# Splitting 80 weight pieces instead of 64 during the attention, in place and in four tiles

## The chip, the cores and the metric

The kernel runs on one core of a Trainium2 chip. The metric is the device time of one execution in microseconds (us), as the median of several runs. Engines are named TensorE (PE in the rows), VectorE (DVE), ScalarE (ACT), GpSimd (POOL) and SyncE (SP, which only issues DMAs); PEld is TensorE's weight load.

## The reference

One layer of a hybrid encoder is applied to a prompt of 1024 tokens and to a sample of 256, each behind 16 learned tokens. The core of it:

```
p = rms_norm(h) @ w_in
c_q, c_kv, k_rope, u = split(p)
o_attn = mla(c_q, c_kv, k_rope, ...)      # 4 heads, softmax over all keys
o_hy   = hyena(u, conv_w, filters, bias)  # order 2: z = x_n * (conv(z, f_n) + bias_n * z)
mix = concat(rms_norm(o_attn), rms_norm(o_hy)) @ w_o
h = h + rms_norm(mix)
m = square(relu(rms_norm(h) @ w_ff1)) @ w_ff2
h = h + rms_norm(m)
```

The widths are 1024 for the model and 4096 for the MLP. All is float32, so `w_o`, `w_ff1` and `w_ff2` are the large weights.

## The kernel before

A float32 product is made as three TensorE products of rounded numbers (`mm3`, L257 to L261): high by high, high by low, low by high. For a weight piece of 128x512 numbers (256 KB) ScalarE casts the high part (`hi`, L267), and GpSimd or VectorE subtracts it from the piece for the low part (`lo`, L270). L273 and L276 are the helpers for other elementwise work of VectorE and GpSimd.

Three stages follow one another. The first makes the projections and the filters (until about 395 us). The second is the attention (to about 612 us), with the sample's convolution in its last units and behind it (to about 690 us). The third is the prompt's hyena convolution, into which the sample's output projection and MLP are woven, and then the prompt's own output projection and MLP.

The attention runs in units, one for 128 queries of one head: 4 heads by 10 query tiles, 8 of the prompt and 2 of the sample. A unit i issues the scores of its tile on TensorE, the row maximum `nmx` on VectorE (L994) and the exponential `prob` on ScalarE (L999). Between these stand the transposes of unit i - 1's probabilities, whose high part `pth` is cast by ScalarE and whose low part `ptl` is subtracted by VectorE, in two groups of 128x512 and a third of 128x128. Two tiles of queries make a pair; their weighted sum `po` is made in parts in the following units, and its result `ot` is stored (`oa`). Steps of the next head's projections (`kh`, `pv`) fill the rest.

Beside it, `presplit` (L361 to L389) makes low parts of weight pieces that the sample path will use later: 16 of `w_o`, then of `w_ff1` and `w_ff2` in the order of their use. SP loads a piece (`pre_raw`, L370), ScalarE casts the high part, GpSimd subtracts the low part, and SP stores the low part to DRAM (`lo_...`, L375). High and low part share a tile, `pre_lo`, of which there are two, so a cast waits until the store of the piece two before has landed. Each unit from the first to the 32nd takes two steps, so 64 pieces are done after 32 units. Later, `ring` (L391) brings each weight piece of the sample path: for a piece with a stored low part it loads the piece and the low part (`w_lo` from DRAM) and casts the high part; for any other it loads the piece and lets GpSimd subtract (`w_lo<-w_raw,w_hi`).

On TensorE, ScalarE and VectorE the attention's instructions keep the order in which the code writes them (`pin`, L1161), except for the sample's convolution (`loose`, L1150). GpSimd's and SP's instructions are placed by a scheduler.

Of the kernel before, what the change touches and what calls it, by code (L numbers as in the profile page):

```python
# [13 lines left out]
F32 = mybir.dt.float32  # L14
F32R = mybir.dt.float32r
# [6 lines left out]
P = 128  # L22
# [154 lines left out]
def mk(ap, dims):  # L177
    return bass.AP(tensor=ap.tensor, offset=ap.offset, ap=[ap.ap[0]] + [list(d) for d in dims])


def f(ap):
    return ap.bitcast(F32)
# [15 lines left out]
def run(gen):  # L198
    for _ in gen:
        pass  # L200
# [32 lines left out]
class Builder:  # L233
# [127 lines left out]
    def presplit(self, pool, n):  # L361
        nc = self.nc
        keys = list(self.sample_pieces())[:n]
        raws, last = {}, None

        def load(k):
            if k < n:
                raw = raws[k] = pool.tile([P, 512], F32, name="pre_raw", bufs=2)
                src = self.piece(*keys[k])
                nc.sync.dma_start(raw.rearrange("p (a b) -> p a b", a=4) if len(src.shape) == 3 else raw, src)  # L370

        def store():
            if last is not None:
                d = self.d_lo[last[0]] = self.dr.tile([P, 512], F32, name="lo_" + "_".join(map(str, last[0])))
                nc.sync.dma_start(d, f(last[1]))  # L375

        load(0)
        load(1)
        yield
        for k in range(n):  # L380
            raw = raws.pop(k)
            t = pool.tile([P, 512], F32R, name="pre_lo", bufs=2)
            self.hi(t, raw)
            self.lo(t, raw, t, nc.gpsimd)
            store()
            last = keys[k], t
            load(k + 2)
            yield
        store()  # L389

    def ring(self, pool, src, bufs, rp=None, every=0, key=None):  # L391
        nc = self.nc
# [503 lines left out]
    def phase_b(self):  # L896
        tc, nc, a = self.tc, self.nc, self.a
# [3 lines left out]
        with ExitStack() as st:  # L901
# [5 lines left out]
            wk = self.pool(st, "b_work", 2)  # L907
# [122 lines left out]
            def weigh(h, t, qp, pth, ptl, rcs):  # L1030
                vh, vl = t[4:]
                nb, b0 = (8, 0) if qp < 4 else (2, 8)
                po = pv.tile([P, 512], F32, name="po", bufs=1)
                o = po[:, :256]
                for b in range(nb):
                    if b == nb // 2:
                        yield
                    self.mm3(o, vh[:, b0 + b], vl[:, b0 + b], pth[:, b], ptl[:, b], b == 0, False)
                b = 8 if qp < 4 else 10
                self.mm3(o, vh[:, b], vl[:, b], pth[:, 8], ptl[:, 8], False, True)  # L1040
                for i in range(2):
                    nc.tensor.transpose(po[:, 256 + i * 128:384 + i * 128], mk(rcs[i], [[0, 128]]), self.ident)
                yield
                rb = wk.tile([P, 256], F32, name="rb")
                nc.scalar.copy(rb, po[:, 256:])
                ot = wk.tile([P, 256], F32, name="ot")
                self.tt(ot, o, rb, ALU.mult)
                (nc.gpsimd if h >= self.dbg.get("oq", 4) else nc.sync).dma_start(self.d_oa[h][:, qp * 256:qp * 256 + 256], ot)
                yield
# [4 lines left out]
            with self.hp(4):  # L1054
                self.hi(krh[0:64], self.ka[0:64])
                self.lo(krl[0:64], self.ka[0:64], krh[0:64])
                raw, rk = stage(TM), stage(T)
                nc.sync.dma_start(rk[64:128], self.ka[0:64])
                nc.sync.dma_start(raw[64:128], self.qr[0:64])
                self.hi(krh[64:128], rk[64:128])  # L1060
                self.lo(krl[64:128], rk[64:128], krh[64:128])
                self.hi(qst[0][0:64], self.qr[0:64])
                self.hi(qst[0][64:128], raw[64:128])
                self.lo(qst[0][64:128], raw[64:128], qst[0][64:128])
                self.ropes.close()
                hps.append(self.pool(st, "b_head1"))
                pre_st = st.enter_context(ExitStack())
                pre = self.presplit(self.pool(pre_st, "b_pre"), 64)
                next(pre)
                for _ in range(self.dbg.get("n6", 6)):  # L1070
                    next(prep, None)
# [15 lines left out]
            n = len(units)  # L1087
# [4 lines left out]
            for i in range(n + 3):  # L1092
                start = len(nc.cur_bb.bb.instructions)
                sm = tn = nothing
                if i < n:
                    h, qt = units[i]
                    if i % 10 == 2 and h + 1 < NH:
                        for _ in prep:
                            pass
                        prep = head_prep(h + 1, heads[h + 1]) if h else early  # L1100
                    prob[i] = []
                    sm = softmax(heads[h], h, qt * 128, qt < 8, sets[qt % 2], reads[qt % 2], prob[i])
                if i == 33:

                    run(pre)
                    pre_st.close()
                    self.low.close()
                    self.wr = self.pool(self.rest, "f_w", 4, side="right")
                    sz = self.pool(self.sz_stack, "sz", 1, side="right")
                    self.conv_constants()  # L1110
                    conv = self.hyena_sample(cp, sz, lambda: pv.tile([P, 512], F32, name="pv"))
                next(sm, None)
                self.loose(conv)
                if 0 < i <= n:
                    h, qt = units[i - 1]
                    pair = (i - 1) // 2
                    if qt % 2 == 0:
                        pts[pair] = (wk.tile([P, 9, 256], F32R, name="pth"), wk.tile([P, 9, 256], F32R, name="ptl"), [])
                    p, rc = prob.pop(i - 1)
                    pts[pair][2].append(rc)  # L1120
                    tn = turn(p, sets[qt % 2], reads[qt % 2], qt < 8, *pts[pair][:2], qt % 2)
                next(tn, None)
                self.loose(conv)
                next(sm, None)
                if i >= 3 and i % 2 == 1:
                    h, qt = units[i - 3]
                    weighing = weigh(h, heads[h], qt // 2, *pts.pop((i - 3) // 2))
                next(weighing, None)
                if i > 0:
                    next(pre, None)  # L1130
                next(tn, None)
                self.loose(conv)
                if i % 2 == 0:
                    next(weighing, None)
                next(prep, None)
                if i > 0:
                    next(pre, None)
                if i == 0:
                    next(prep, None)
                if self.dbg.get("c4", 0):  # L1140
                    self.loose(conv)
                if i == n + 2:
                    a0 = len(nc.cur_bb.bb.instructions)
                    run(conv)
                    if self.dbg.get("lo", 1):
                        self.free.update(x.name for x in nc.cur_bb.bb.instructions[a0:])
                if self.dbg.get("pin", 1):
                    self.pin(start)
# [760 lines left out]
```

## Time and profile before

| | |
|---|---|
| median of 3 runs | 1961.19 us (1959.61 to 1962.14) |
| profiled execution | 1959.85 us, its span 1958.1 us |
| TensorE busy | 1787.0 us, 91% |
| VectorE busy | 1189.3 us, 61% |
| ScalarE busy | 773.8 us, 40% |
| GpSimd busy | 648.1 us, 33% |
| `w_lo` subtractions on GpSimd | 292, 414.8 us |
| `pre_lo` subtractions on GpSimd | 64, 81.9 us |

Busy times are sums over the whole span. They say which engine is nearest to its bound on average; which one sets the end in a stage is read from that stage's waits. An instruction's bracket tells how long its engine sat idle before it, and what ended that.

### The profile page before, as it was taken

Reading aid. Unit: us, or ns where it says so; the run is one execution under the profiler, and the core shown is the slowest. Engines: PE = TensorE matmul, PEld = TensorE weight load, DVE = VectorE, ACT = ScalarE, POOL = GpSimd, SP = SyncE. Lnnn points to the kernel's source line nnn. Section 1 sums busy time; section 2 is a strip of 40 time slices with the busy share of each in tenths; the row PEclk is TensorE's granted clock in tenths of the full one; section 3 lists DMA queues with packets and bytes.
Section 4 is the critical chain, followed back from the end, with each engine's and each line's share of the span. In section 5 each row is a group of like instructions: output and inputs, shape, how many; then the busy total and the mean of one; then the engine's idle time right before and its main releaser. Section 6 shows DMA issues by size and latency. Waiting matters only on the chain. (4 is left out here: it accounts for less than half of the span.)

```text
span 1958.1 us, 26574 instructions
## 1 busy us (share of the span) xinstructions
PE 1787.0 (91%) x9806; PEld 1566.5 (80%) x9806; DVE 1189.3 (61%) x1958; ACT 773.8 (40%) x1378; POOL 648.1 (33%) x556
## 2 busy tenths in 40 slices
PE   7999999889887987998889899899999999999996
PEld 6898999778776776887769778677888888888885
DVE  6589885755455858999752865764343333333346
ACT  6444343365554444332254565554322222222232
POOL 3221212344452210124466762234422222222234
PEclk9999998999999989999989989899999999999998
DMA  4454535356566266764443564335211111111104
GB/s 164 149 178 151 178 111 177 95 170 192 176 202 218 78 235 208 258 218 142 154 147 121 178 225 147 120 112 192 96 50 44 44 43 44 50 52 55 59 1 140
DMA packets 173669, 263.10 MB, mean 134 GB/s; under 512 B 14491, under 2 KB 85089, under 8 KB 173411
## 3 DMA queue, kind: packets, MB, share of 16 engines
q1 hardware_dynamic: 164952, 242.38, 38.4%
q0 software_dynamic: 5872, 17.06, 2.9%
q10 hardware_dynamic: 2714, 1.96, 0.3%
q8 instruction: 77, 1.26, 0.3%
q14 instruction: 54, 0.43, 0.1%
HBM read 202.51 MB, written 56.18 MB: 132 GB/s over the span
## 5 line engine op out<-in xcount | busy, mean ns | idle before, releaser
L270 POOL TENSOR_TENSOR w_lo<-w_raw,w_hi 128x512 fp32r<-128x512 f32 x292 | 414.8, 1433 | 705.3 <-ACT w_hi L267 638.7
L267 ACT CAST w_hi<-w_raw 128x512 fp32r<-128x512 f32 x388 | 237.8, 619 | 444.2 <-PE p L260 289.8
L259 PE MATMUL p<-a2h,w_hi 128*128 128x512 f32 (+1 forms) x784 | 283.8, 362 | 15.1 <-ACT w_hi L267 7.8
L259 PE MATMUL p<-sh,w_hi 128*128 128x512 f32 (+1 forms) x800 | 285.6, 361 | 11.0 <-DVE acc L273 6.0
L260 PE MATMUL p<-sl,w_hi 128*128 128x512 f32 (+1 forms) x800 | 283.4, 354 | 8.4 <-DVE sl L270 8.4
L261 PE MATMUL p<-a2h,w_lo 128*128 128x512 f32 (+1 forms) x784 | 281.6, 359 | 7.6 <-POOL w_lo L270 7.6
L261 PE MATMUL p<-sh,w_lo 128*128 128x512 f32 (+1 forms) x800 | 283.6, 355 | 0.0
L260 PE MATMUL p<-a2l,w_hi 128*128 128x512 f32 (+1 forms) x784 | 279.9, 357 | 0.3
L273 DVE TENSOR_TENSOR acc<-acc,p 128x512 f32<-128x512 f32 (+1 forms) x284 | 184.8, 656 | 147.4 <-PE p L261 147.0
L259 PEld LDWEIGHTS p<-sh,w_hi 128*128 128x128 f32 x800 | 154.5, 194 | 35.6 <-ACT sh L267 6.1
L259 PEld LDWEIGHTS p<-a2h,w_hi 128*128 128x128 f32 x784 | 151.8, 194 | 38.1 <-ACT w_hi L267 10.7
L260 PEld LDWEIGHTS p<-sl,w_hi 128*128 128x128 f32 x800 | 155.5, 194 | 31.7 <-DVE sl L270 11.0
L261 PEld LDWEIGHTS p<-a2h,w_lo 128*128 128x128 f32 x784 | 152.1, 194 | 31.5 <-POOL w_lo L270 9.8
L261 PEld LDWEIGHTS p<-sh,w_lo 128*128 128x128 f32 x800 | 155.3, 194 | 21.0
L260 PEld LDWEIGHTS p<-a2l,w_hi 128*128 128x128 f32 x784 | 151.9, 194 | 22.5 <-DVE a2l L276 0.7
L276 DVE SCALAR_TENSOR_TENSOR rl<-p,rs 128x512 f32<-128x512 f32 (+1 forms) x66 | 44.5, 674 | 199.7 <-PE p L261 199.6
L1769 ACT ACTIVATE rl<-rl 128x512 f32<-128x512 f32 (+1 forms) x66 | 40.8, 619 | 236.4 <-DVE rl L276 236.4
L259 PE MATMUL pp<-ah,w_hi 128*128 128x432 f32 x336 | 123.6, 368 | 0.0
L261 PE MATMUL pp<-ah,w_lo 128*128 128x432 f32 x336 | 122.0, 363 | 0.0
L260 PE MATMUL pp<-al,w_hi 128*128 128x432 f32 x336 | 121.9, 363 | 0.0
L270 POOL TENSOR_TENSOR pre_lo<-pre_raw,pre_lo 128x512 fp32r<-128x512 f32 x64 | 81.9, 1282 | 102.7 <-ACT pre_lo L267 102.3
L270 DVE TENSOR_TENSOR ptl<-sset,pth 128x512 fp32r<-128x512 f32 (+2 forms) x112 | 59.0, 527 | 84.0 <-ACT pth L267 83.8
(383 smaller groups left out, 3793.8 us busy)
## 6 DMA issues: line engine op xcount, KB each, us to landing
w_raw<-in_w_ff SPq DMA_DIRECT2D x292, 256.0 KB, 2.9
w_raw<-in_w_o SPq DMA_DIRECT2D x64, 256.0 KB, 3.2
fct<-in_c_f POOLq DMA_DIRECT2D x32, 384.0 KB, 4.2
pre_raw<-in_w_ff SPq DMA_DIRECT2D x48, 256.0 KB, 3.1
lo_w_ff<-pre_lo SPq DMA_DIRECT2D x48, 256.0 KB, 3.6
w_lo<-lo_w_ff SPq DMA_DIRECT2D x48, 256.0 KB, 4.2
w_raw<-in_w_in SPq DMA_DIRECT2D x32, 256.0 KB, 2.6
k<-spec SPq DMA_DIRECT2D x8, 1024.0 KB, 4.7
```

Source lines behind the costliest of these rows:

```text
L259: mm(out, lhsT=ah, rhs=bh, start=start, stop=False)
L260: mm(out, lhsT=ah, rhs=bl, start=False, stop=False)
L261: return mm(out, lhsT=al, rhs=bh, start=False, stop=stop).ins
L267: return self.nc.scalar.copy(out, src).ins
L270: return (eng or self.nc.vector).tensor_tensor(out, src, f(hi), op=ALU.subtract).ins
L273: (eng or self.nc.vector).tensor_tensor(out, a, b, op=op)
L276: (eng or self.nc.vector).scalar_tensor_tensor(out, x, s, y, op0=op0, op1=op1)
L1769: nc.scalar.activation(r, r, AF.Square)
```

## The change

Pieces are loaded into four `pre_raw` tiles instead of two. The high part goes into a tile of its own, `pre_hi`, of which there is one. The low part is written over the loaded piece and stored from there. The list of pieces grows from 64 to 80: the sixteen new ones are the eight of `w_ff2` in group 2 and eight of `w_ff1` in group 4. In every even unit from the second on a third step is taken, directly behind the exponential. `rb` and `ot` get one buffer each.

```diff
-                raw = raws[k] = pool.tile([P, 512], F32, name="pre_raw", bufs=2)
+                raw = raws[k] = pool.tile([P, 512], F32, name="pre_raw", bufs=4)
...
-        def store():
-            if last is not None:
-                d = self.d_lo[last[0]] = self.dr.tile([P, 512], F32, name="lo_" + "_".join(map(str, last[0])))
-                nc.sync.dma_start(d, f(last[1]))
+        def store(k):
+            if k in raws:
+                d = self.d_lo[keys[k]] = self.dr.tile([P, 512], F32, name="lo_" + "_".join(map(str, keys[k])))
+                nc.sync.dma_start(d, raws.pop(k))
...
-            raw = raws.pop(k)
-            t = pool.tile([P, 512], F32R, name="pre_lo", bufs=2)
-            self.hi(t, raw)
-            self.lo(t, raw, t, nc.gpsimd)
-            store()
-            last = keys[k], t
+            t = pool.tile([P, 512], F32R, name="pre_hi", bufs=1)
+            self.hi(t, raws[k])
+            self.lo(raws[k], raws[k], t, nc.gpsimd)
+            store(k - 1)
             load(k + 2)
             yield
-        store()
+        store(n - 1)
...
-                rb = wk.tile([P, 256], F32, name="rb")
+                rb = wk.tile([P, 256], F32, name="rb", bufs=1)
                 nc.scalar.copy(rb, po[:, 256:])
-                ot = wk.tile([P, 256], F32, name="ot")
+                ot = wk.tile([P, 256], F32, name="ot", bufs=1)
...
-                pre = self.presplit(self.pool(pre_st, "b_pre"), 64)
+                pre = self.presplit(self.pool(pre_st, "b_pre"), 80)
...
                 self.loose(conv)
                 next(sm, None)
+                if i > 0 and i % 2 == 0:
+                    next(pre, None)
                 if i >= 3 and i % 2 == 1:
```

On ScalarE, in the middle of the attention, the rows of an odd and an even unit were, from one exponential on:

```order
L999 ACTIVATE prob,sm<-sset_3786,nmx 128x1040
L267 CAST pre_lo<-pre_raw 128x512
L267 CAST pth<-sset_3785 128x128
L267 CAST pre_lo<-pre_raw 128x512
L267 CAST pth<-sset_3786 128x4x128 x2
L999 ACTIVATE prob,sm<-sset_3785,nmx 128x1040
L267 CAST pre_lo<-pre_raw 128x512
L267 CAST pth<-sset_3786 128x128
L1045 COPY rb<-po 128x256
L267 CAST kh<-pv 128x432
L267 CAST pre_lo<-pre_raw 128x512
```

In the changed program an even unit has, at the same place:

```order
L267 CAST pth<-sset_3786 128x4x128 x2
L997 ACTIVATE prob,sm<-sset_3785,nmx 128x1040
L267 CAST pre_hi<-pre_raw 128x512 x2
L267 CAST pth<-sset_3786 128x128
L1043 COPY rb<-po 128x256
L267 CAST kh<-pv 128x432
L267 CAST pre_hi<-pre_raw 128x512
```

Two casts of pieces instead of one stand between the exponential and the third cast of the probabilities.

On SP, at pieces 24 to 27 counted from 0 (`lo_w_ff_4_0` is the DRAM copy of the low part of piece 24, and the last number is a tile's), loads and stores took turns:

```order
L375 DMA lo_w_ff_4_0_4864<-pre_lo 128x512
L370 DMA pre_raw<-in_w_ff 128x512
L375 DMA lo_w_ff_4_1_4923<-pre_lo 128x512
L920 DMA stage<-qr_96 64x1280
L370 DMA pre_raw<-in_w_ff 128x512
L1048 DMA oa_106<-ot 128x256
L375 DMA lo_w_ff_5_0_4944<-pre_lo 128x512
L370 DMA pre_raw<-in_w_ff 128x512
L375 DMA lo_w_ff_5_1_5001<-pre_lo 128x512
```

From the store of piece 26 (`lo_w_ff_5_0`) on, the changed program has:

```order
L375 DMA lo_w_ff_5_0_4795<-pre_raw 128x512
L370 DMA pre_raw<-in_w_ff 128x512 x2
L375 DMA lo_w_ff_5_1_4810<-pre_raw 128x512
L375 DMA lo_w_ff_6_0_4833<-pre_raw 128x512
L1046 DMA oa_105<-ot 128x256
L375 DMA lo_w_ff_6_1_4890<-pre_raw 128x512
L370 DMA pre_raw<-in_w_ff 128x512
L370 DMA pre_raw<-in_w_ff 128x4x128 x2
L375 DMA lo_w_ff_7_0_4906<-pre_raw 128x512
L375 DMA lo_w_ff_7_1_4948<-pre_raw 128x512
L370 DMA pre_raw<-in_w_ff 128x4x128 x2
```

The loads between the stores of pieces 26 and 27 are those of pieces 29 and 30, and the three behind the store of piece 29 those of pieces 31 to 33. Five pieces pass in two units, in groups.

On GpSimd, at the end of the prompt's hyena (`cpr` and `bl` are work of the hyena), 18 subtractions for the sample path stood ahead of the last `cpr`:

```order
L273 TENSOR_TENSOR cpr<-ends,cf 128x256
L270 TENSOR_TENSOR w_lo<-w_raw,w_hi 128x512 x4
L273 TENSOR_TENSOR bl<-xf,kt 128x512
L270 TENSOR_TENSOR w_lo<-w_raw,w_hi 128x512 x3
L273 TENSOR_TENSOR cpr<-ends,cf 128x256
L270 TENSOR_TENSOR w_lo<-w_raw,w_hi 128x512
L273 TENSOR_TENSOR bl<-xf,kt 128x512
L270 TENSOR_TENSOR w_lo<-w_raw,w_hi 128x512
L273 TENSOR_TENSOR bl<-xf,kt 128x512
L270 TENSOR_TENSOR w_lo<-w_raw,w_hi 128x512 x3
L273 TENSOR_TENSOR bl<-xf,kt 128x512
L270 TENSOR_TENSOR w_lo<-w_raw,w_hi 128x512 x6
```

Behind these rows come the last `cpr` and 242 further subtractions. The changed program has:

```order
L273 TENSOR_TENSOR cpr<-ends,cf 128x256
L273 TENSOR_TENSOR bl<-xf,kt 128x512
L273 TENSOR_TENSOR cpr<-ends,cf 128x256
L273 TENSOR_TENSOR bl<-xf,kt 128x512 x3
L273 TENSOR_TENSOR cpr<-ends,cf 128x256
L270 TENSOR_TENSOR w_lo<-w_raw,w_hi 128x512 x244
```

Sixteen subtractions are gone, and the other two stand behind the last `cpr`.

## Rows read from the trace of the kernel before

**Rows 1.** Busy us by stretch: PE, PEld, DVE, ACT, POOL, PEclk, DMA share, GB/s.

```profile
399.00:612.00 213.00, 179.78 (x1202) 165.61 (x1201) 104.51 (x194) 119.40 (x259) 99.55 (x104) 0.93 0.62 192
612.00:690.00 78.00, 68.53 (x419) 57.75 (x419) 59.65 (x134) 36.62 (x70) 15.87 (x32) 1.00 0.40 135
690.00:897.00 207.00, 185.18 (x1164) 168.08 (x1165) 178.76 (x319) 80.89 (x147) 33.73 (x33) 0.94 0.67 219
897.00:948.00 51.00, 35.75 (x238) 32.74 (x237) 51.00 (x59) 13.53 (x24) 33.65 (x22) 0.92 0.46 147
...
1250.00:1958.00 708.00, 680.38 (x3151) 563.23 (x3149) 308.39 (x470) 204.01 (x353) 209.27 (x166) 0.98 0.22 71
```

**Rows 2.** Waits in 399 to 612 us: total us, times, longest us.

```profile
DVE ptl L270 <- ACT pth L267: 77.5, 73, 4.8
ACT pre_lo L267 <- DMA lo_w_ff<-pre_lo: 45.4, 26, 5.6
...
PE sset L259 <- DVE ptl L270: 31.0, 21, 4.6
...
ACT pre_lo L267 <- DMA lo_w_o<-pre_lo: 15.8, 10, 2.6
```

**Rows 3.** Instructions of a unit: start us, us, ..., [idle before, releaser].

```profile
468.44 1.24 DVE L994 TENSOR_REDUCE nmx<-sset 128x1 f32<-128x1040 f32 x1 [1.59 <-PE sset L989]
...
473.12 0.39 PE L259 MATMUL sset<-kh,qnh 128*128 128x272 f32 x1 [0.38 <-DVE ptl L270]
...
474.06 1.24 DVE L994 TENSOR_REDUCE nmx<-sset 128x1 f32<-128x1040 f32 x1
```

**Rows 4.** Instructions of a unit with a store wait, and SP's issues.

```profile
505.09 0.62 ACT L267 CAST pre_lo<-pre_raw 128x512 fp32r<-128x512 f32 x1 [1.36 <-DMA lo_w_ff<-pre_lo]
505.79 1.27 POOL L270 TENSOR_TENSOR pre_lo<-pre_raw,pre_lo 128x512 fp32r<-128x512 f32 x1 [3.08 <-ACT pre_lo L267]
...
506.25 0.60 PE L259 MATMUL sset<-kh,qnh 128*128 128x272 f32 x1 [3.09 <-DVE ptl L270]
...
507.09 0.38 SPq L370 DMA_DIRECT2D pre_raw<-in_w_ff  x1
...
507.51 0.51 SPq L375 DMA_DIRECT2D lo_w_ff<-pre_lo  x1
```

**Rows 5.** Row maxima of the units: ns min/median/max, first and last start.

```profile
L994 DVE TENSOR_REDUCE nmx<-sset x33: 429/1240/1242, 395.7 to 608.8; 128x1 f32<-128x1040 f32 x25, 128x1 f32<-128x272 f32 x8
```

**Rows 6.** TensorE's waits in 897 to 948 us.

```profile
PE ips L1675 <- DVE bv L273: 11.8, 3, 5.5
...
PE p L259 <- DVE acc L273: 1.5, 1, 1.5
...
PE p L261 <- POOL w_lo L270: 0.9, 1, 0.9
```

**Rows 7.** GpSimd's subtractions in 897 to 948 us: busy us, mean ns | idle.

```profile
L270 POOL TENSOR_TENSOR w_lo<-w_raw,w_hi 128x512 fp32r<-128x512 f32 x17 | 27.8, 1656 | 11.2 <-ACT w_hi L267 11.1
```

**Rows 8.** Two instruction groups of VectorE there: start us, us.

```profile
899.87 5.11 DVE L273 TENSOR_TENSOR bl<-bpq 128x512 f32<-128x512 f32 x3
...
904.90 0.68 DVE L273 TENSOR_TENSOR bv<-bv 128x512 f32<-128x512 f32 x1
```

**Rows 9.** GpSimd's subtractions in the attention: ns min/median/max, first and last start.

```profile
L270 POOL TENSOR_TENSOR pre_lo<-pre_raw,pre_lo x64: 1262/1282/1301, 400.0 to 611.6; 128x512 fp32r<-128x512 f32 x64
```

**Rows 10.** DMA issues in 400 to 612 us: KB, us to landing.

```profile
pre_raw<-in_w_ff SPq DMA_DIRECT2D x48, 256.0 KB, 3.1
lo_w_ff<-pre_lo SPq DMA_DIRECT2D x47, 256.0 KB, 3.6
```

**Rows 11.** ScalarE's two longest waits for a store.

```profile
584.34 0.62 ACT L267 CAST pre_lo<-pre_raw 128x512 fp32r<-128x512 f32 x1 [4.23 <-DMA lo_w_ff<-pre_lo]
...
591.22 0.62 ACT L267 CAST pre_lo<-pre_raw 128x512 fp32r<-128x512 f32 x1 [5.61 <-DMA lo_w_ff<-pre_lo]
```

More of the change, by code (lines that the diff above doesn't have):

```diff
@@ L363, in presplit @@
         keys = list(self.sample_pieces())[:n]
-        raws, last = {}, None
+        raws = {}
         def load(k):
             if k < n:
-                raw = raws[k] = pool.tile([P, 512], F32, name="pre_raw", bufs=2)
+                raw = raws[k] = pool.tile([P, 512], F32, name="pre_raw", bufs=4)
                 src = self.piece(*keys[k])
                 nc.sync.dma_start(raw.rearrange("p (a b) -> p a b", a=4) if len(src.shape) == 3 else raw, src)
-        def store():
-            if last is not None:
-                d = self.d_lo[last[0]] = self.dr.tile([P, 512], F32, name="lo_" + "_".join(map(str, last[0])))
-                nc.sync.dma_start(d, f(last[1]))
+        def store(k):
+            if k in raws:
+                d = self.d_lo[keys[k]] = self.dr.tile([P, 512], F32, name="lo_" + "_".join(map(str, keys[k])))
+                nc.sync.dma_start(d, raws.pop(k))
         load(0)
```

## The prediction

> **What bounds the kernel now.** I read first the busy times by stretch, then the waits of the attention, then its instructions one by one, and last the stretch of the hyena in which the first pieces outside the set of 64 are split.
>
> After 1250 us TensorE is busy for 680.4 of 708 us [rows 1]. Nothing the change touches runs there, so I leave that stage as it is. In the attention (399 to 612) TensorE is busy for 179.8 of 213 us, so 33.2 us are idle, and its largest wait is for DVE's low part of the probabilities, 31.0 us in 21 places [rows 1, 2]. That wait is inherited: DVE waits for ScalarE's cast of the probabilities, and ScalarE stood still for 45.4 + 15.8 = 61.2 us in 36 places until a store of low parts had landed, because a cast of a weight piece needs one of two `pre_lo` tiles back [rows 2]. Two instances show the pattern. In a unit where ScalarE does not wait for a store ahead of the third cast of the probabilities, one row maximum follows the other after 474.06 - 468.44 = 5.62 us, and the score matmul waits 0.38 us for the low part [rows 3]. At 505.09 the cast of a piece waited 1.36 us for a store, and 1.2 us later the score matmul had waited 3.09 us [rows 4]. The 33 row maxima from 395.7 to 608.8 make 32 intervals of 213.1 / 32 = 6.66 us [rows 5]. At 5.62 each they would be 179.8 us, which is TensorE's busy time. So the stalls are worth 33.3 us, and a unit without them is bound by TensorE.
>
> Later, at 897 to 948, DVE is busy for all 51.0 us and TensorE for 35.75, so TensorE idles 15.25 us, 11.8 of it in three waits for DVE's `bv` [rows 1, 6]. This is where GpSimd starts the `w_lo` subtractions of pieces 64 and up: 17 of them, at 1656 ns mean [rows 7]. DVE operations with two SBUF operands take 5.11 / 3 = 1.70 us beside them and 0.68 us at 904.90 [rows 8].
>
> **The change: the attention.** 80 pieces in 32 units instead of 64 means one more step in each of 16 even units, directly behind the exponential. ScalarE there does exp, cast, cast, third cast of the probabilities. There is only one `pre_hi` tile, so the second cast waits for GpSimd's subtraction of the first: cast to subtraction 505.79 - 505.09 = 0.70 us, subtraction 1.28 us [rows 4, 9], and about 0.05 us from GpSimd's end to ScalarE's start (an estimate): 2.03 us. The path has no slack at this place, for the score matmul already waits 0.38 us in the undisturbed unit and TensorE is full otherwise. So I take the whole 2.03 us, 16 times: +32.5 us. The subtraction has the same operands and sizes; I cost writing it in place at nothing, since GpSimd is busy for 99.6 of 213 us [rows 1]. One buffer each for `rb` and `ot` costs nothing while their last use lies a pair back, some 13 us; only an output store that takes as long as that to land would hold VectorE.
>
> Against this stand the old stalls of 33.3 us. The wait for a store is no longer ScalarE's: high parts do not go to DRAM, and the low part sits in the piece's tile, of which there are four. The wait moves to SP: the load of piece k needs the store of piece k-4 to have landed, and as the new order shows, stores stand behind such loads in SP's one queue (store 26, load 30, store 27, store 28, output, store 29, loads 31 to 33). In place of the store wait, ScalarE can then only wait for a late load. Per pair of units (five pieces) that ring closes as: cast and subtraction 2.02, store landing 3.6, next issue 0.42, the following store landing 3.6, load landing 3.1 [rows 4, 10], together 12.7 us. A pair on ScalarE and TensorE takes 5.62 + 5.62 + 2.03 = 13.27. On medians SP keeps up by 0.5 us a pair.
>
> What stays of stalls, s, I bound by 0 and by 33.3 (the ring as tight as now). Two waits that came with the loads of the constants, of 4.23 and 5.61 us [rows 11], stay in any ring of a few buffers: 9.8 us. With a margin of 0.5 us and landings that scatter I add 0.4 us for each of 16 pairs, 6.4 us (an estimate). That gives s = 16.2. The attention changes by 32.5 - 33.3 + 16.2 = +15.4 us, and with the ends of s by -0.8 to +32.5.
>
> A rule of the Trainium skill ("DMA: Bandwidth & Descriptors", section Anatomy of one DMA — SWDGE path) would price a transfer at 2.0 us plus its bytes at 436 GB/s, which is 2.6 us for 256 KB (estimate). The rows have 3.1 and 3.6, on SP's queue and with 192 GB/s of other traffic. By the rule the ring would take 10.2 us a pair, the margin would be 3 us, and only the constants' waits would stay: 32.5 - 33.3 + 9.8 = +9 us in the attention instead of +15.4, and a median of 1955.7, on the way to the second rival below.
>
> **The change: the hyena.** 16 of the 17 subtractions at 897 to 948 disappear, since these pieces' low parts now come by a load. In the changed program all remaining `w_lo` stand behind the last `cpr` of the hyena on GpSimd. Each of the 16 cost DVE up to 1.70 - 0.68 = 1.02 us [rows 8], 16.3 us in all, while DVE is what TensorE waits for. TensorE's 15.25 us of idle time caps the gain, and its waits for the last sums and weights (1.5 us for `acc` among them) [rows 6] need not go. I take -14.5 us, between -17 (18 `w_lo` stand ahead of the last `cpr` before; the two that are not removed move behind it and give back 1 us each) and -3 (DVE gets free, but TensorE then waits for the 16 extra `w_lo` loads or for ScalarE).
>
> Here too the Trainium skill has a rule ("SBUF — State Buffer", section Who interferes with whom): a DVE instruction with two SBUF inputs and a GpSimd instruction that reads SBUF block each other for a whole instruction. The trace agrees in kind: 1.70 against 0.68 here, while in the attention, where DVE reads scores from PSUM, the same subtraction stays at 1262 to 1301 ns [rows 9]. With a full block of 1.28 us each the 16 would be worth 20.5 us, and the rows give 16.3.
>
> **Sum.** +15.4 - 14.5 = +0.9 us. The steps of the sample convolution behind the attention stand in another order; I count them at 0, within 3 us either way, since TensorE is busy there for 68.5 of 78 us [rows 1]. So 1959.85 + 0.9 = 1960.75 us for the profiled execution. That execution is 1.34 us under the median of 1961.19, so the forecast for the median is 1962.1, rounded to 1962.
>
> **Rivals.**
> *The ring is slower than the pair (slower).* Three transfers lie in series in each cycle. If each takes 0.55 us more than its median, because 80 loads and 80 stores now share the time of 64, a pair takes 12.7 + 1.65 = 14.35 us, and 16 of them 229.6. With the constants' 9.8 us on top the attention is 239.4 - 213.1 = +26.3 us longer, and with -14.5 from the hyena the sum is +11.8: 1973. For it: every load waits for a landing, and in SP's queue a load that waits holds back the next store. Against it: at 192 GB/s the DMA engines are busy for 0.62 of this stretch [rows 1], so there is room. It decides from 13.27 us a pair.
> *The stalls all but vanish (faster).* Pairs take 13.27 us, 212.3 in all, with 5 us of stalls: +4.2 in the attention and -15 in the hyena, so -10.8, and 1950.4. For it: with four tiles a piece's store has more time to land, and the constants' waits may fall into the deeper ring. Against it: those two waits are far longer than the mean of 61.2 / 36 = 1.7 us.
> *The hyena's gain does not arrive (slower).* +15.4 - 3 = +12.4, so 1973.6. For it: the 16 pieces now need a second load each on SP's queue, in a stage that moves 147 to 219 GB/s [rows 1]. Against it: TensorE waits there 0.9 us for `w_lo` and 11.8 for `bv` [rows 6].
>
> **How the numbers follow.** About 0.2%, 3.9 us, is what a measurement of this kernel can tell from no change. The balance (1962, own range 1955 to 1969) gets 0.42: 0.24 within 0.2%, 0.09 on either side. The slow ring gets 0.28, the vanished stalls 0.23, the missing hyena gain 0.07 (0.05 slower, 0.02 same). Faster: 0.09 + 0.23 = 0.32. Same: 0.24 + 0.02 = 0.26. Slower: 0.09 + 0.28 + 0.05 = 0.42. The range goes from a little under the faster rival, 1949, to a little over the slower ones, 1976.
>
> **What the new profile would show.** Right: the 32 intervals of the row maxima sum to about 228 us, with even units some 2 us longer than odd ones; ScalarE's `pre_hi` casts wait 16 times for GpSimd, about 1.3 us each; its waits for stores are gone; loads make it wait for some 16 us in all. At the hyena, GpSimd's `w_lo` group counts 276 instead of 292, the 0.68 us operations of DVE keep their time until the last `cpr`, and TensorE's wait for `bv` falls by two thirds. Wrong: intervals that sum to 213 or less (a ring with more slack), or to 240 (a ring bound by SP); even units that are not longer (a slack on ScalarE's path that I have not seen); TensorE waiting on `w_lo` loads in the hyena for over 3 us.

## The result, and the profile after

The changed kernel takes 1970.05 us, the median of 10 runs (1965.03 to 1976.96). The kernel before took 1957.91 us in 10 runs beside them (1951.75 to 1962.14). The ratio is 1.006, 95% interval 1.0041 to 1.0078, so the change makes the kernel some 12 us slower. The profiled execution took 1976.45 us (span 1974.7), near the slow end of these runs, so single stages of it are compared below with other kernels that contain the same stage.

The attention first. The row maxima of the changed kernel:

```profile
L992 DVE TENSOR_REDUCE nmx<-sset x33: 430/1241/1245, 398.3 to 631.5; 128x1 f32<-128x1040 f32 x25, 128x1 f32<-128x272 f32 x8
```

The 32 intervals sum to 233.2 us, against 213.1 [rows 5]. This stretch is called "the attention" from here on. Its waits (engine, line, waited for: total us, times, longest us):

```profile
PE sset L259 <- DVE ptl L270: 47.0, 26, 7.9
ACT pre_hi L267 <- POOL pre_raw L270: 46.5, 43, 3.8
...
ACT pre_hi L267 <- DMA pre_raw<-in_w_ff: 20.8, 9, 6.7
...
ACT pre_hi L267 <- DMA pre_raw<-in_w_o: 2.6, 1, 2.6
```

ScalarE's 61.2 us of waits for stores [rows 2] are gone. In their place stand 46.5 us for GpSimd and 23.4 us for loads. TensorE waits 47.0 us for the low part of the probabilities, against 31.0. Ahead of `rb` and `ot`, of which there is now one each, no engine waits. An ordinary even unit, instruction by instruction (start us, us, ..., [idle before, releaser]):

```profile
478.36 1.24 DVE L992 TENSOR_REDUCE nmx<-sset 128x1 f32<-128x1040 f32 x1 [0.98 <-PE sset L987]
...
481.88 0.62 ACT L267 CAST pre_hi<-pre_raw 128x512 fp32r<-128x512 f32 x1
482.57 1.26 POOL L270 TENSOR_TENSOR pre_raw<-pre_raw,pre_hi 128x512 f32<-128x512 f32 x1 [2.09 <-ACT pre_hi L267]
483.87 0.62 ACT L267 CAST pre_hi<-pre_raw 128x512 fp32r<-128x512 f32 x1 [1.38 <-POOL pre_raw L270]
...
485.03 0.59 PE L259 MATMUL sset<-kh,qnh 128*128 128x272 f32 x1 [2.48 <-DVE ptl L270]
...
486.57 1.24 DVE L992 TENSOR_REDUCE nmx<-sset 128x1 f32<-128x1040 f32 x1 [0.58 <-PE sset L987]
```

The second cast starts 483.87 - 481.88 = 1.99 us behind the first, 1.38 us of it waiting for the one high tile. The score matmul waits 2.48 us where it waited 0.38 [rows 3], and the unit takes 8.21 us.

The matmul itself then takes 0.59 us where it took 0.39 [rows 3]. TensorE had stood idle from 482.55; its granted clock fell to 0.5 (1.2 GHz, the lower of its two levels) at 484.8 and was back at 1.0 (2.4 GHz) from 488.2. In unit 6, shown below, it was at 0.5 from 443.8 to 450.6, and there too it fell inside a long wait. The stretch of the attention, columns as in [rows 1]:

```profile
399.00:630.00 231.00, 184.53 (x1195) 170.45 (x1194) 104.21 (x193) 128.00 (x273) 118.76 (x118) 0.90 0.64 207
```

The mean granted clock is 0.90, where it was 0.93 before [rows 1]. From the first row maximum to the last, TensorE is busy for 186.2 us in the changed kernel and for 181.8 before, with practically the same number of matmuls (1206 and 1207). So of the 20.1 us by which the attention grew, 4.4 are TensorE's own work taking longer at a lower clock, and the rest is idle time.

In units 6, 16 and 26 GpSimd makes a `qst` for the next head; this is unit 6:

```profile
438.97 2.91 POOL L270 TENSOR_TENSOR qst<-stage,qst 64x1280 fp32r<-64x1280 f32 x1
...
439.21 0.62 ACT L267 CAST pre_hi<-pre_raw 128x512 fp32r<-128x512 f32 x1
...
442.33 1.26 POOL L270 TENSOR_TENSOR pre_raw<-pre_raw,pre_hi 128x512 f32<-128x512 f32 x1
...
443.62 0.62 ACT L267 CAST pre_hi<-pre_raw 128x512 fp32r<-128x512 f32 x1 [3.79 <-POOL pre_raw L270]
...
444.78 0.59 PE L259 MATMUL sset<-kh,qnh 128*128 128x272 f32 x1 [4.24 <-DVE ptl L270]
```

The `qst` subtraction starts 0.24 us before the first cast, the piece's subtraction waits for its end, the second cast waits for that subtraction, and TensorE then waits 4.24 us. These three units take 11.9, 11.3 and 10.5 us.

The two groups of GpSimd's subtractions, from the page (busy us, mean ns | idle before):

```profile
L270 POOL TENSOR_TENSOR w_lo<-w_raw,w_hi 128x512 fp32r<-128x512 f32 x276 | 387.4, 1417 | 705.1 <-ACT w_hi L267 641.4
...
L270 POOL TENSOR_TENSOR pre_raw<-pre_raw,pre_hi 128x512 f32<-128x512 f32 x80 | 102.6, 1282 | 87.4 <-ACT pre_hi L267 85.5
```

16 `w_lo` subtractions are gone, and the subtraction in place costs the same as before (mean 1282 ns; before 81.9 / 64 = 1.28 us). Then the hyena, 690 to 1010 us, TensorE's waits, and one group of VectorE:

```profile
PE p L261 <- DMA w_lo<-lo_w_ff: 6.4, 2, 6.2
...
PE ips L1675 <- DVE bv L273: 1.9, 4, 0.7
```

```profile
921.90 1.89 DVE L273 TENSOR_TENSOR bl<-bpq 128x512 f32<-128x512 f32 x3
```

Before, the same stretch had:

```profile
PE ips L1675 <- DVE bv L273: 15.0, 7, 5.5
```

The waits for `bv` fell from 15.0 to 1.9 us; three `bl<-bpq` take 1.89 us, and took 5.11 [rows 8]. A wait of 6.2 us for the load of a low part is new.

### The profile page after: what moved, and what is told of

Same layout as the page of the kernel before. It is cut to its first block, busy times and chain, and to the rows that moved or that the text cites. A ratio compares the mean times of both kernels' runs of the same rounds, so it can differ in the third digit from the quotient of the medians.

```text
span 1974.7 us, 26663 instructions
## 1 busy us (share of the span) xinstructions
PE 1792.0 (91%) x9806; PEld 1572.7 (80%) x9806; DVE 1170.4 (59%) x1958; ACT 782.8 (40%) x1394; POOL 644.0 (33%) x556
## 4 chain that ended last, share of the span: by engine, by line
PE 60%; DVE 16%; DMA 9%; issue 5%; POOL 5%; ACT 4%; SPq 0%; POOLq 0%; DVEq 0%; ACTq 0%
PE p L259 12%; PE p L260 12%; PE p L261 12%; POOL pre_raw L270 3%; DVE bl L273 2%; PE ips L1675 2%; DMA lo_w_ff<-pre_raw 2%; PE pp L259 2%; PE pp L260 2%; PE pp L261 2%; PE wps L259 2%; PE wps L261 2%; PE wps L260 2%; DMA pre_raw<-in_w_ff 1%; POOL w_lo L270 1%
## 5 line engine op out<-in xcount | busy, mean ns | idle before, releaser
L270 POOL TENSOR_TENSOR w_lo<-w_raw,w_hi 128x512 fp32r<-128x512 f32 x276 | 387.4, 1417 | 705.1 <-ACT w_hi L267 641.4
L260 PEld LDWEIGHTS p<-sl,w_hi 128*128 128x128 f32 x800 | 155.8, 195 | 29.5 <-DVE sl L270 10.9
L270 POOL TENSOR_TENSOR pre_raw<-pre_raw,pre_hi 128x512 f32<-128x512 f32 x80 | 102.6, 1282 | 87.4 <-ACT pre_hi L267 85.5
```

Of the source, the lines that this page charges most:

```text
L260: mm(out, lhsT=ah, rhs=bl, start=False, stop=False)
L270: return (eng or self.nc.vector).tensor_tensor(out, src, f(hi), op=ALU.subtract).ins
```

## The experiments

Each kernel was timed beside the kernel before, and its ratio is to that one. The median of the kernel before lay between 1957.91 and 1959.80 us in the five sessions, so kernels of different sessions are better compared by ratio. The attention's length is that of the one profiled execution.

| kernel | attention, us | median, us | ratio (95%) |
|---|---|---|---|
| before | 213.1 | 1957.91 | 1 |
| changed | 233.2 | 1970.05 | 1.0060 (1.0041 to 1.0078) |
| e1, 64 pieces, new tiles | 194.2 | 1939.75 | 0.9895 (0.9876 to 0.9914) |
| e2, two high, three raw | 246.7 | 1982.01 | 1.0118 (1.0102 to 1.0133) |
| e3, 16 not used | 231.9 | 1978.33 | 1.0096 (1.0083 to 1.0109) |
| e4, 80 in the old tiles | 270.8 | 2005.09 | 1.0236 (1.0219 to 1.0254) |
| e5, third high elsewhere | 228.6 | 1959.39 | 1.0002 (0.9987 to 1.0018) |
| e6, qst on VectorE | 239.3 | 1975.14 | 1.0088 (1.0064 to 1.0112) |
| e7, kt on another queue | 232.3 | 1966.90 | 1.0032 (1.0014 to 1.0049) |
| e8, third step behind | 225.8 | 1962.07 | 1.0012 (0.9992 to 1.0032) |
| e9, SP for weights only | 231.6 | 1969.76 | 1.0052 (1.0035 to 1.0069) |
| e10, 64, two high, three raw | 204.4 | 1947.29 | 0.9937 (0.9917 to 0.9958) |
| e11, 72 pieces | 211.8 | 1947.31 | 0.9939 (0.9918 to 0.9960) |
| e12, 77 pieces | 225.3 | 1959.79 | 0.9992 (0.9977 to 1.0008) |

**e1: the new tiles without the third step.**

```diff
-                pre = self.presplit(self.pool(pre_st, "b_pre"), 80)
+                pre = self.presplit(self.pool(pre_st, "b_pre"), 64)
...
-                if i > 0 and i % 2 == 0:
-                    next(pre, None)
```

> The new tiles (four pre_raw, one pre_hi, low part in place) with 64 pieces and without the third step; the hyena stage is as before. Measured so far, from the 2nd to the 34th row maximum: 213.1 us before, 233.2 us after. Theory (the third cast of a piece costs, by the single high tile; the new ring itself has more room than the old): ScalarE's waits for stores go, some 10 us of late loads and some 6 us by the three qst subtractions on GpSimd stay, so 196 to 203 us in the attention and 10 to 15 us less than before in all (ratio 0.992 to 0.995). Rival (SP's ring of loads behind stores sets the pace): 210 to 215 us, and the time of before.

Row maxima, and the waits from 396 to 591 us:

```profile
L992 DVE TENSOR_REDUCE nmx<-sset x33: 431/1242/1245, 396.5 to 590.7; 128x1 f32<-128x1040 f32 x25, 128x1 f32<-128x272 f32 x8
```

```profile
ACT pre_hi L267 <- POOL pre_raw L270: 23.7, 29, 2.3
...
PE sset L259 <- DVE ptl L270: 18.9, 15, 3.9
...
ACT pre_hi L267 <- DMA pre_raw<-in_w_ff: 13.8, 4, 5.0
```

The attention is 18.9 us shorter than before, a little under the theory's range, and the kernel is 1% faster than the kernel before, more than expected. The rival, a ring as slow as the old one, falls. This is the fastest kernel of the study: the tiles are a gain, and the 16 further pieces are what loses.

Of the 39.0 us between this attention and that of the changed kernel, 28.1 are TensorE's waits for the low part (47.0 - 18.9). The other 10.9 are TensorE's own work: busy for 175.3 us here and 186.2 there, with 1206 matmuls each, at a mean granted clock of 0.94 here and 0.90 there.

**e2: two high tiles and three for the piece.**

```diff
-                raw = raws[k] = pool.tile([P, 512], F32, name="pre_raw", bufs=4)
+                raw = raws[k] = pool.tile([P, 512], F32, name="pre_raw", bufs=3)
...
-            t = pool.tile([P, 512], F32R, name="pre_hi", bufs=1)
+            t = pool.tile([P, 512], F32R, name="pre_hi", bufs=2)
```

> 80 pieces as in the changed kernel, but two pre_hi tiles and three pre_raw (the same bytes). Theory (single high tile): ScalarE's 45.5 us of waits for GpSimd fall below 10; 1.4 us less in each of 16 even units, 2 to 3 us less in each of the three units with a qst subtraction, so 205 to 215 us in the attention if loads keep up, and 15 to 25 us less than the changed kernel. Rival (SP's ring): a load must wait for the store of the piece three before instead of four, ScalarE's waits for loads grow from 23 us to over 45, and the attention stays at 233 us or grows.

Waits from 397 to 645 us:

```profile
ACT pre_hi L267 <- DMA pre_raw<-in_w_ff: 58.8, 31, 5.3
...
PE sset L259 <- DVE ptl L270: 57.9, 32, 4.9
...
ACT pre_hi L267 <- DMA pre_raw<-in_w_o: 11.4, 7, 3.9
...
ACT pre_hi L267 <- POOL pre_raw L270: 7.5, 8, 1.4
```

My theory missed: the waits for GpSimd went as it said, but the loads' 70.2 us took their place, and the kernel is slower than the changed one. With three tiles SP's ring binds; this is what that rival looks like, and the changed kernel with 23.4 us in 10 waits is not like it. Both kinds of tile are short at five pieces in two units; no run has four and two together.

**e3: the low parts of the 16 further pieces are made, but not used.**

```diff
-        if key in self.d_lo:
+        if key in set(list(self.sample_pieces())[:64]):
```

> The attention of the changed kernel with its 80 pieces, but the sample path does not use the low parts of the pieces 64 to 79 and lets GpSimd subtract them as before. This leaves the attention's cost alone. Theory (the hyena gives back 8 us: 11.5 us of waits for bv less 6.2 us of a w_lo load that comes late, and 3 us besides): 7 to 10 us slower than the changed kernel, TensorE's waits for bv near 13 us again and none for w_lo loads over 1 us in that stage. Rival (the gain did not arrive): the time of the changed kernel within 3 us.

TensorE's waits from 690 to 1010 us:

```profile
PE ips L1675 <- DVE bv L273: 11.8, 8, 4.4
...
PE p L261 <- POOL w_lo L270: 3.4, 3, 1.7
```

The waits for `bv` are back, and no `w_ff` low part comes late. The kernel is 8.3 us slower than the changed one by medians, 0.0036 of 1958 us, or 7 us, by ratios. So the hyena does give something back, and the attention's cost alone is about 19 us.

**e4: 80 pieces in the old tiles** (an edit of the kernel before).

```diff
-                pre = self.presplit(self.pool(pre_st, "b_pre"), 64)
+                pre = self.presplit(self.pool(pre_st, "b_pre"), 80)
...
                 next(sm, None)
+                if i > 0 and i % 2 == 0:
+                    next(pre, None)
```

> 80 pieces with the third step in even units, but with the old tiles (two pre_raw, two pre_lo that hold high and then low part). Theory (the old ring needs 6.1 us for two pieces, so 15.3 us for five): 245 to 255 us in the attention, ScalarE's waits for stores over 80 us, 12 to 22 us slower than the changed kernel. Rival (the tiles do not matter, the third cast does): 228 to 238 us and the time of the changed kernel.

Waits from 396 to 670 us:

```profile
ACT pre_lo L267 <- DMA lo_w_ff<-pre_lo: 89.5, 48, 4.8
...
ACT pre_lo L267 <- DMA lo_w_o<-pre_lo: 18.9, 10, 3.4
```

108.4 us of waits for stores, and the kernel 35 us slower than the changed one, beyond the range that I gave. The rival that tiles do not matter falls: at 80 pieces the new tiles are worth 37.6 us in the attention, at 64 pieces 18.9.

**e5: the third step's high part in a tile of the probabilities.** The tile that waits is taken away for one of the three pieces.

```diff
-            t = pool.tile([P, 512], F32R, name="pre_hi", bufs=1)
+            t = self.third() if self.third else pool.tile([P, 512], F32R, name="pre_hi", bufs=1)
...
                 if i > 0 and i % 2 == 0:
+                    self.third = lambda: pw.tile([P, 512], F32R, name="pre_h3", tag="prob", bufs=3)
                     next(pre, None)
+                    self.third = None
```

> The changed kernel, but the high part of the third step's piece goes into one of the three tiles of the probabilities' ring, so that the cast behind it need not wait for GpSimd; four pre_raw tiles and one pre_hi stay. The attention took 233.2 us in the changed kernel and 194.2 with 64 pieces. Theory (the wait for the single high tile is the price): ordinary even units lose 1.4 of their 2.0 us, the three units with a qst subtraction 2 to 4 us each; ScalarE's waits for GpSimd fall from 45.5 us to 10 to 25; attention 205 to 215 us; 18 to 28 us less than the changed kernel, 1942 to 1952. Rival (SP's ring of loads is next): ScalarE's waits for loads grow from 23 us to over 40, attention 225 us or more, at most 8 us gained.

Row maxima of units 2 to 4, and waits from 396 to 625.5 us:

```profile
403.73 1.24 DVE L994 TENSOR_REDUCE nmx<-sset 128x1 f32<-128x1040 f32 x1 [1.32 <-PE sset L989]
...
409.87 1.24 DVE L994 TENSOR_REDUCE nmx<-sset 128x1 f32<-128x1040 f32 x1 [0.20 <-PE sset L989]
...
416.11 1.24 DVE L994 TENSOR_REDUCE nmx<-sset 128x1 f32<-128x1040 f32 x1 [0.25 <-PE sset L989]
```

```profile
ACT pre_hi L267 <- POOL pre_raw L270: 31.7, 23, 4.4
...
ACT pre_hi L267 <- DMA pre_raw<-in_w_ff: 31.1, 17, 6.6
...
ACT pre_hi L267 <- DMA pre_raw<-in_w_o: 4.8, 3, 2.1
```

Both expectations failed in part. Unit 2 takes 6.14 us, where it took 8.1 in the changed kernel and 5.9 with 64 pieces. Units 4, 12, 14 and 24 are alike: 0.3 to 0.5 us above e1, where the changed kernel is 1.7 to 2.6 above. There the wait for the high tile is most of the price; in units 8, 10, 18, 20 and 28 the edit wins nothing. And the attention as a whole is only 4.6 us shorter. Units 6 and 7, 16 and 17, 26 and 27 take 17.8 to 19.2 us together, where they took 16.2 to 18.0, and ScalarE waits 35.9 us for loads instead of 23.4. The kernel is 0.6% faster than the changed one, as fast as before.

**e6: the qst subtraction on VectorE.**

```diff
-                self.lo(qst[h][64:128], raw[64:128], qst[h][64:128], nc.gpsimd)
+                self.lo(qst[h][64:128], raw[64:128], qst[h][64:128], nc.vector)
```

> The changed kernel with the qst subtraction (2.9 us on GpSimd, three times) on VectorE. Theory (it delays the subtraction of a piece, and through the single high tile ScalarE): the units 6, 16 and 26, of 11.9, 11.3 and 10.5 us, fall to 8 to 9.5 us, 5 to 9 us less in all; ScalarE's longest wait for GpSimd falls from 3.8 to under 2.5 us. Rival (these units are long by the next head's projections): unchanged units, or longer, since VectorE takes the work, and the time of the changed kernel within 3 us.

```profile
437.77 1.49 DVE L270 TENSOR_TENSOR qst<-stage,qst 64x1280 fp32r<-64x1280 f32 x1 [6.29 <-POOL qst L919]
```

Units 6, 16 and 26 fall to 7.7 us, but units 5, 15 and 25 rise to 11.4 to 13.1: VectorE, in the order of the code, stood 6.29 us until the copy on GpSimd was done. The edit put a new wait where it took one away, and its time decides nothing.

**e7 and e9: what holds the load of a low part in the hyena.** e7 moves the `kt` loads to GpSimd's queue, e9 the `xg` loads and `oh` stores too.

```diff
-                self.q("lk").dma_start(t, self.d_k[o][h][:, :, mq * 2:mq * 2 + 2])
+                nc.gpsimd.dma_start(t, self.d_k[o][h][:, :, mq * 2:mq * 2 + 2])
```

> The changed kernel with the hyena's kt loads on GpSimd's queue instead of SP's. Theory (SP stood 3.6 us at a kt load that waits for a buffer and 3 us at stores of the hyena, with w_lo loads queued behind): TensorE's wait of 6.2 us for a w_lo load becomes under 3 us, 3 to 7 us less than the changed kernel. Rival (the load is late by its own landing, or GpSimd's queue now holds the hyena's products): the time of the changed kernel within 3 us, or slower.

```diff
-                self.q("lx").dma_start(xs[:, cc], self.d_u[1 + o][2 * h + cc][:, :C_S])
+                nc.gpsimd.dma_start(xs[:, cc], self.d_u[1 + o][2 * h + cc][:, :C_S])
...
-                    self.q("oh").dma_start(self.d_oh[ct][:, :LP], outs[:, cc, :LP])
+                    nc.gpsimd.dma_start(self.d_oh[ct][:, :LP], outs[:, cc, :LP])
```

> The changed kernel with the hyena's kt and xg loads and its oh stores on GpSimd's queue, so that SP has only weight pieces in that stage. With kt alone moved, SP stood 6.8 us at an oh store that waits for VectorE, and TensorE waited 7.4 us for a w_lo load. Theory (whatever of the hyena waits on SP holds the w_lo loads behind it): no wait of TensorE for a w_lo load over 2 us from 690 to 1010 us, 4 to 7 us less there. Rival (the load waits for its own buffer or bandwidth): a wait of 5 us or more stays.

In the changed kernel SP issues the late loads behind the hyena's transfers, and TensorE waits for them:

```profile
940.23 0.32 SPq L1689 DMA_DIRECT2D oh<-outs  x1
...
942.60 1.97 SPq L397 DMA_DIRECT2D w_lo<-lo_w_ff  x4
...
949.89 0.58 PE L261 MATMUL p<-a2h,w_lo 128*128 128x256 f32 x1 [6.20 <-DMA w_lo<-lo_w_ff]
```

In e9, at the same place:

```profile
941.88 0.39 PE L261 MATMUL p<-a2h,w_lo 128*128 128x256 f32 x1 [1.83 <-DMA w_lo<-lo_w_ff]
...
946.06 0.39 PE L261 MATMUL p<-a2h,w_lo 128*128 128x256 f32 x1 [2.48 <-DMA w_lo<-lo_w_ff]
```

Its waits from 690 to 1010 us:

```profile
PE p L261 <- DMA w_lo<-lo_w_ff: 5.9, 4, 2.5
PE ips L1675 <- DVE bv L273: 5.6, 5, 3.1
```

In e7 the longest wait stayed, at 7.4 us, so `kt` was not the whole cause. In e9 it is gone, so the hyena's transfers on SP made that one long wait. But four waits of 5.9 us together stand where two of 6.4 us stood, and the theory (none over 2 us) missed. The time does not follow either: e9 is at 1.0052 where the changed kernel is at 1.0060. TensorE waits 5.6 us for `bv` instead of 1.9; that the late load had lain in part where VectorE would have been late is likely, but not shown. e7 is at 1.0032, a little better than the changed kernel, with intervals that overlap and no wait that accounts for it.

**e8: the third step behind the third cast of the probabilities.**

```diff
                 next(sm, None)
-                if i > 0 and i % 2 == 0:
-                    next(pre, None)
...
                 if i % 2 == 0:
                     next(weighing, None)
+                if i > 0 and i % 2 == 0:
+                    next(pre, None)
```

> The changed kernel with the third step of even units moved behind the third cast of the probabilities. Theory (the wait for the high tile costs most where the score matmul's low part is behind it): the score matmul's waits for the low part fall from 45 us, attention 215 to 228 us, 5 to 18 us less. Rival (three casts through one high tile take 3 x 2.02 = 6.1 us in any order, and the next unit's first cast then stands behind the last): 230 to 236 us in the attention and the time of the changed kernel within 4 us.

```profile
PE sset L259 <- DVE ptl L270: 39.2, 28, 6.7
```

The attention is 7.4 us shorter, within the theory's range, and the kernel 0.5% faster than the changed one. TensorE's waits for the low part fall from 47.0 to 39.2 us. So the place of the step accounts for 7.4 of the 39.0 us over e1, and 31.6 stay wherever it stands; this run does not show what they are made of.

**e10: 64 pieces with two high tiles and three for the piece** (the edits of e1 and e2).

> 64 pieces without the third step, with two pre_hi and three pre_raw tiles instead of one and four. With one and four the attention took 194.2 us and ScalarE waited 23.7 us for GpSimd and 15.1 us for loads. Theory (with four pieces in two units either ring fits; the high tile's wait matters little where no third cast stands): waits for GpSimd under 8 us, waits for loads 20 to 40 us, attention 194 to 206 us, 0 to 10 us more than with one and four. Rival (the high tile is what binds at 64 too): attention under 190 us and 5 us or more below it.

ScalarE waits 2.7 us for GpSimd and 41.8 for loads, and the attention is 10.2 us longer than in e1: the theory's case, with both a little over its ranges. At the same bytes, four tiles and one are better than three and two at 64 pieces as at 80.

**e11: 72 pieces, a third step in every fourth unit.**

```diff
-                pre = self.presplit(self.pool(pre_st, "b_pre"), 80)
+                pre = self.presplit(self.pool(pre_st, "b_pre"), 72)
...
-                if i > 0 and i % 2 == 0:
+                if i > 0 and i % 4 == 0:
```

> 72 pieces: the third step in every fourth unit only (units 4, 8, ... 32), four pre_raw and one pre_hi. Theory (each third step costs by itself, 39.0 us for 16 of them, and the hyena gives back 8.3 us for 16): with 8 of them 16 to 22 us over the 194.2 us of the attention with 64 pieces, 3 to 6 us given back, so 10 to 18 us above the 64 pieces in all. Rival (the ring has a threshold, and four and a half pieces in two units still fit): attention under 204 us, within 5 us of the 64 pieces.

Eight third steps cost 17.6 us in the attention, 2.2 each, as expected. The kernel is only 7.6 us above e1 by medians, 8.6 by ratios, where 10 to 18 were expected; so eight pieces would give back 9 to 10 us, about what sixteen do. By the length of the hyena's stage (below) eight give 6.5 us and sixteen 10.4. TensorE's waits for `bv` are down to 5.6 us already. How much the last eight win is left open. The ring shows no threshold between 64 and 80: the first eight cost 17.6 us in the attention, the next eight 21.4.

**e12: 77 pieces, no third step in units 6, 16 and 26.**

```diff
-                pre = self.presplit(self.pool(pre_st, "b_pre"), 80)
+                pre = self.presplit(self.pool(pre_st, "b_pre"), 77)
...
-                if i > 0 and i % 2 == 0:
+                if i > 0 and i % 2 == 0 and i % 10 != 6:
```

> 77 pieces: the third step in all even units but 6, 16 and 26, where GpSimd also makes a qst (4.2 us). These units took 11.9, 11.3 and 10.5 us in the changed kernel and 6.8 us each with 64 pieces. Theory (there the wait for the single high tile is a wait for the qst work, 4.4 us a unit and not 2.0): units 6, 16 and 26 back to 6.5 to 7.5 us, attention 13 us below that of the changed kernel (218 to 222 us), 9 to 14 us less in all with 3 pieces more for the hyena. Rival (every third step costs the same 2.4 us): 7 us below in the attention, 4 to 7 us less in all, and the price turns up in the units beside.

The row maximum at 437.92 is that of unit 7 and ends unit 6:

```profile
435.95 2.93 POOL L270 TENSOR_TENSOR qst<-stage,qst 64x1280 fp32r<-64x1280 f32 x1
...
437.92 1.24 DVE L992 TENSOR_REDUCE nmx<-sset 128x1 f32<-128x1040 f32 x1 [0.19 <-PE sset L987]
...
440.67 0.62 ACT L267 CAST pre_hi<-pre_raw 128x512 fp32r<-128x512 f32 x1 [3.66 <-POOL pre_raw L270]
```

Units 6, 16 and 26 are back at 6.8 us, as the theory had it. But the wait for the `qst` work, 3.66 us, now stands in front of unit 7's casts, and that unit takes 9.0 us instead of 6.1. The attention is 7.9 us shorter, near the rival's size, and the time is 10 us shorter by medians and 13 by ratios, the theory's. So the high tile does make ScalarE wait for the `qst` work, with or without a third step there. Of the 13.4 us that units 6, 16 and 26 win, units 7, 17 and 27 lose 5.0 again, so the third steps in these three cost 8.4 us net, 2.8 each. Why the kernel as a whole wins more than its attention is not shown.

## Why the prediction was right, and which of its terms were off

The sign of the likeliest side and the range were right: slower had the largest chance, and 1970.05 lies within 1949 to 1976. The number 1962 was 8 us low against the median, and 11 us low as a change (+12 instead of +1), 1 us outside the likeliest case's own range. The terms, one by one:

- **The stalls of the old tiles go, and s = 16.2 us stay.** e1 has the new tiles alone, though with four pieces in two units and not five: 194.2 - 179.8 = 14.4 us stay, near 16.2. The constants' waits came: 10.7 us of late loads in units 30 and 31, where I had put 9.8. The scattered landings did not come as such: one late load of 3.0 us is all that is left for them. Beside it ScalarE waits 23.7 us for GpSimd, which I had not counted in s. Not all of that reaches TensorE, which waits 18.9 us in all.
- **The third step costs 2.03 us, 16 times.** The wait that it was worked out from is there: 1.99 us between the two casts in the ordinary unit shown above, and e5 shows in five units that the single tile makes most of the price. As a sum it was too small: from e1 to the changed kernel the attention grows by 39.0 us, not 32.5 (37.4 to 38.1 in the three other kernels with this attention: e3, e7 and e9). And it is not the same in every unit. Units 6, 16 and 26 grow by 13.4 us, because GpSimd has 4.2 us of `qst` work there and I had taken it as free whenever a cast ends. Unit 30 grows by 6.0 us with a wait of 6.7 us for a late load, which e10 has there without any third step (6.0 us). The other twelve grow by 18.9 us, 1.6 each, and some of them hardly at all: unit 18 not, unit 28 by 0.6. The odd units grow by 0.7 us in all. That 32.5 came so near is in part luck.
- **TensorE's own speed.** The sum has no term for it, and no reason why. 10.9 of the 39.0 us are TensorE's instructions taking longer at a mean granted clock of 0.90 instead of 0.94.
- **The hyena gives 14.5 us.** This term was mis-sized most. e3 measures it alone: 7 to 8 us. The stage's length gives about 10: from the last row maximum to the last product of the prompt's `w_o` it is 619.0 to 622.6 us (mean 620.8) in the four kernels that use 64 low parts (before, e1, e3, e10), and 607.2 to 615.1 (mean 610.4) in the eight that use 80. The part on VectorE came as written: it is busy for 435.3 us between these points, before for 452.4, and the waits for `bv` fell from 15.0 to 1.9 us. What failed is that TensorE would get nearly all of it back. What I priced only as the lower bound, and named as a sign of being wrong, came as well: low parts that land late, 6.2 us, behind the hyena's own transfers in SP's queue. But e9, without that long wait, is no faster, so what keeps the rest from TensorE stays open.
- **Sum.** By the measured sizes: 38 - 33.3 + 14.4 = +19 us for the attention and -7 to -10 for the hyena, so +9 to +12; measured are +12.

The direction was luck in part. Of the 0.42 that I gave to slower, 0.28 were the slow ring's, which did not come. It gave nearly the right time (1973) by a wrong mechanism: e2 is what that ring does, and the changed kernel's loads wait a third as long. The missing hyena gain was half true. The vanished stalls did not come: even with 64 pieces 14.4 us stay, not 5.

The page "DMA: Bandwidth & Descriptors" of the Trainium skill (section Anatomy of one DMA — SWDGE path) gives its price for transfers of the GpSimd path: 2.6 us for 256 KB, an estimate. These transfers go by SP's queue; the changed kernel's stores are nearer to it than the rows that I used. Its DMA issues, KB each and median us to landing:

```profile
pre_raw<-in_w_ff SPq DMA_DIRECT2D x64, 256.0 KB, 3.2
lo_w_ff<-pre_raw SPq DMA_DIRECT2D x64, 256.0 KB, 2.4
```

Stores land in 2.4 us, not 3.6 [rows 10], and loads in 3.2. With 2.4 twice in place of 3.6 the ring of a pair takes 10.4 us by my own sum, well under the pair's 13.3. That alone does not show why SP did not bind: in e2 the stores land in 2.0 us, and ScalarE waits 70.2 us for loads.

## What to carry to other kernels

Price a helper step by the tile it must get back, and ask of the engine that frees the tile what else it does in those units: a wait of 1.4 us for GpSimd became 3.8 us in unit 6, where GpSimd had other work. Ask too what a longer wait does to the speed of the engine that waits: here TensorE's own work took 10.9 us more. Split an edit with two parts before judging it: here the tiles alone win 1.05% (e1) and the longer list loses 1.65%. When work is moved from an engine to a DMA, look at what its queue waits for just ahead of where the load is needed.

## What was not expected of the hardware

The landing time of a 256 KB store was 3.6 us in one kernel and 2.4 us in the other, for the same bytes on the same queue with 192 and 207 GB/s of traffic in that stretch. The tiles are not the reason: e1, with the new ones, has 3.6 us too, and e2 has 2.0. No run here shows the reason. And breaking up TensorE's longest wait in the hyena (6.2 us, e9) did not shorten the kernel: shorter waits for late loads stayed, and the waits for VectorE grew by 3.7 us.
